# Splitting every fourth half unit of streamed weights with two GpSimd DMAs in a two-block transformer kernel

## Chip, cores and metric

The kernel runs on one core of one Trainium2 chip. The metric is the device time of that core in microseconds, as the median over runs of the same program. All inputs lie in the chip's memory before the program starts, and the output is written back there.

## What is computed

The reference applies two transformer blocks to 256 tokens of width 2048, in float32. Block 1 has differential attention and retention side by side, then cross attention to 256 memory tokens, then a gated feed-forward. Block 2 has spatial gating and a gated linear recurrence side by side, then a feed-forward with a short convolution. All the large work is the matrix products with the weights:

```python
def first_block(x, mem, ...):
    h = rmsnorm(x, norm_mix_g[l]);  proj = h @ w_in[l]
    ...                                   # differential attention, retention -> mixed
    x = x + mixed @ w_o[l]
    hx = rmsnorm(x, norm_x_g[l]);  hm = rmsnorm(mem, norm_mem_g[l])
    xq, xk, xv = hx @ w_xq[l], hm @ w_xk[l], hm @ w_xv[l]
    ...                                   # softmax attention -> xo
    x = x + xo @ w_xo[l]
    hf = rmsnorm(x, norm_ffn_g[l])
    x = x + (silu(hf @ w_gate[l]) * (hf @ w_up[l])) @ w_down[l]
    return rmsnorm(x, norm_f_g)

def second_block(x, ...):
    p = rmsnorm(x, norm1_g[l]) @ w_in[l]
    ...                                   # spatial gating, recurrence -> y
    x = x + y @ w_out[l]
    up = causal_dwconv(rmsnorm(x, norm2_g[l]) @ ffn_w_up[l])
    gate, val = split(up)
    x = x + (gelu(gate) * val) @ ffn_w_down[l]
    return rmsnorm(x, final_g)
```

## The kernel before

Every product is computed with split operands: a float32 value is written as hi + lo, both of type float32r, where hi is the value cast to float32r and lo is what the cast left over. A product then is hi·hi + hi·lo + lo·hi, three matmuls in place of one, added up in PSUM.

The weights are a stream. They lie in memory as 452 units of 1 MB, each 128 partitions by 2048 floats, in the order `seq` in which the GEMMs use them. `fetch` (lines 218 to 226) loads one unit on the SP queue into a tile `w` of the pool `wraw` (3 buffers). `push` (line 228) takes a half unit, 128 by 1024, from it and calls `split` (line 127). There ACT casts it into a tile `wh` of the pool `whi` (line 129), and DVE subtracts `wh` from the raw weights into a tile `wl` of the pool `wlo` (line 130). Each of these two pools has 5 buffers. So half unit n takes the buffers that half unit n−5 had, and can start only when PE has done the last matmul with that one. There are 904 half units; the last 5 are kept in other tiles for a second pass, so 899 go through `wh` and `wl`.

`half` (line 249) is called by the GEMMs for the next half unit and keeps `LOOKAHEAD` = 4 further ones pushed. `gemm_tm` (line 312) has the activations as stationary operand and moves 512 weight columns: for one half unit 4 groups of the three matmuls of `mm3`, lines 145 (hi weights), 146 (lo weights) and 147 (hi weights). `gemm_fm` (line 282) has the weights as stationary operand: 8 matmuls with hi weights against 512 columns (line 297) and 8 with lo weights against 256 (line 301) for one half unit. PSUM holds two groups at a time (`pg`).

Work beside the GEMMs (attention heads, norms, the recurrence) is written as generators, one stage per half unit (`tick`, line 262). A scheduler then sets the order of the instructions on each engine from estimated durations; each engine takes its list strictly in that order and waits where an operand or a buffer is not ready. POOL, the engine of GpSimd, has little to do: inverse square roots by power (line 151), some additions of squares (line 413) and two selections (line 828).

Of the kernel before, what the change touches and what calls it, by code (L numbers as in the profile page):

```python
# [8 lines left out]
F32 = mybir.dt.float32  # L9
F32R = mybir.dt.float32r  # L10
# [12 lines left out]
LOOKAHEAD = 4  # L23
TAIL = 5  # half units at the end whose operands stay for a second pass

# columns of the packed per-feature vectors
_COLS = [
# [17 lines left out]
def tile_kernel(ctx, tc, x, xT, mem, memT, par, alibi, rdecay, ident_d, bc_rows, gm_wsT,  # L45
# [29 lines left out]
    class Pair:  # L75
        """two k-tiles of a split operand: tiles of (hi | lo), or a tile of hi and one of lo"""

# [13 lines left out]
        def fill(self, src, gcols=None):  # L91
            """hi + lo == src * gain; src [P, 2, S] or two of [P, S]"""
            if gcols is None and not self.joined:
                split(self.t[0], self.t[1], src)
            else:
                for k in range(2):
                    split(self.hi(k), self.lo(k), src[:, k, :], None if gcols is None else gcols[k])
            return self
# [6 lines left out]

# [1 line left out]
    pr = cpool.tile([P, NPAR], F32, name="pr")  # L107
# [6 lines left out]
    V.memset(mhalf, -0.5)  # L114
    # the first activation table loads while the first data comes
    A.activation(st(1), mhalf[:, 0:1], AF.Square)
# [8 lines left out]

# [1 line left out]
    def split(hi, lo, src, gcol=None):  # L127
# [7 lines left out]
    def xpose_split(src, c, gcols=None, joined=False):  # L135
        """token-major src[t][:, c:c+256] -> split feature-major pair"""
        pt = sps().rearrange("p (k s) -> p k s", k=2)
        for k in range(2):
            for t in range(2):
                T.transpose(pt[:, k, t * P:(t + 1) * P], src[t][:, c + k * P:c + (k + 1) * P], ident)  # L140
        return Pair(joined).fill(pt, gcols)

    def mm3(out, lh, rh, start, stop):
        """both operands as (hi, lo)"""
        T.matmul(out, lhsT=lh[0], rhs=rh[0], start=start, stop=False)  # L145
        T.matmul(out, lhsT=lh[0], rhs=rh[1], start=False, stop=False)  # L146
        T.matmul(out, lhsT=lh[1], rhs=rh[0], start=False, stop=stop)  # L147
# [6 lines left out]
    class Sq:  # L154
        """sums of squares of token-major rows, piece by piece"""

# [18 lines left out]
    def rows(c):  # L175
        """[P tokens, 2] columns -> [P, 256], the same row in every partition"""
        d = flat(ft())[:, 0:S]
        for t in range(2):
            V.tensor_scalar(d[:, t * P:(t + 1) * P], ident, c[:, t:t + 1], None, ALU.mult)
        ps = sps()  # L180
        T.matmul(ps[:, 0:S], lhsT=ones, rhs=d, start=True, stop=True)
        r = spool.tile([P, S], F32, tag="rows", name=nm("rows"), bufs=3)
        A.copy(r, ps[:, 0:S])
        return r
# [3 lines left out]

# [1 line left out]
    seq = [(w_in_f, 0, u) for u in range(2)]  # L190
# [37 lines left out]
    def push():  # L228
        """one more half unit on its way"""
        w, g, u = seq[pos[1] // 2]  # L230
        h = pos[1] % 2
        if not raws:
            fetch()
        r = raws[0][:, 1024 * h:1024 * h + 1024]
        if h == 1:
            raws.pop(0)
        pos[1] += 1
        if pos[1] > 2 * len(seq) - TAIL:
            # kept until both halves of the tokens have used them
            hi, lo = [flat(rt()) for _ in range(2)], [flat(rt()) for _ in range(2)]  # L240
            for k in range(2):
                split(hi[k], lo[k], r[:, 512 * k:512 * k + 512])
        else:
            hi = whi.tile([P, 1024], F32R, tag="h", name=nm("wh"))
            lo = wlo.tile([P, 1024], F32R, tag="l", name=nm("wl"))
            split(hi, lo, r)
        feed.append((w, g, u, h, hi, lo))
# [10 lines left out]

# [1 line left out]
    bg = []  # L260
# [21 lines left out]
    def gemm_fm(wap, g, acts):  # L282
        """256 output features x 256 tokens: [P, m, (hi parts | lo parts)]"""
        ps = psg.tile([P, 2, 512], F32, tag="g", name=nm("pg"))
# [27 lines left out]
    def gemm_tm(wap, g, acts, k0=0, ps=None, tail=0):  # L312
        """256 tokens (2 banks) x 512 output features; in the last `tail` half units the second
        half of the tokens waits for the function that is returned"""
        if ps is None:
# [39 lines left out]
    def evac_split(ps, c):  # L355
        """token-major, as (hi, lo) for each half of the tokens"""
        res = []
        for t in range(2):
            hi, lo = flat(rt()), flat(rt())
            split(hi, lo, ps[t], need(c, 0)[:, t:t + 1])  # L360
            res.append((hi, lo))
        return res
# [10 lines left out]
    def operands(g, acts, gcols):  # L373
        """columns 512 g of the residual as operands of a GEMM"""
        for p in range(2):
# [4 lines left out]
    def next_in(g, acts, sq, gcols, after=None):  # L380
        """behind a residual update of columns 512 g"""
        if acts is not None:
# [8 lines left out]
    def stats(sq, rc, rr=None):  # L391
        """rstd of the rows as columns, and as a row in every partition"""
        rc[0] = sq.rstd(D)
# [4 lines left out]

    # =================================================================
    # block 1: projections, differential attention, retention  # L400
    # =================================================================
    def load(src, p):
# [4 lines left out]
    def load_split(f, gname, p, sq):  # L407
        a = Pair(True).fill(f, [col(gname, 2 * p + j) for j in range(2)])
        # sum of squares, feature-major
        s = ft()  # L410
# [7 lines left out]
    def col_stats(sq, n):  # L418
        """feature-major squares -> rstd as columns"""
        tot = sps()  # L420
# [10 lines left out]
    def x_gen():  # L431
        # loads (L), weight units (W) and splits (S) in the order in which they start
        n = 0
# [26 lines left out]

    # lambda = exp(q1.k1) - exp(q2.k2) + lam_init
    lam_init = 0.8 - 0.6 * math.exp(-0.3 * 0)
# [17 lines left out]
    def av_stage(pT, v, off):  # L480
        """[q, 256] = P^T.T @ v, causal in blocks of 128, and its sums of squares"""
        po = sps().rearrange("p (t e) -> p t e", t=2)
# [123 lines left out]

    # memory
    hm_a, sqm = [None] * 8, []
# [29 lines left out]

    # =================================================================
    # cross attention  # L640
    # =================================================================
    xk = []
# [6 lines left out]
    for g in range(4):  # L649
        if g == 3:  # L650
            # takes the space of the memory's operands, pair by pair
            spawn(chain([operands(i, hx_a, cols("norm_x_g", 0, 16)) for i in range(4)]))
# [50 lines left out]

    # =================================================================
    # feed-forward 1
    # =================================================================
    gg = cpool.tile([P, 16], F32, name="gg")
# [9 lines left out]
    def second_norm(g):  # L717
        # block 2 takes rmsnorm(x) * norm_f_g and normalises it again
        gf = flat(ft())
# [20 lines left out]

    # =================================================================
    # block 2: spatial gating and recurrent branch
    # =================================================================
    def tok(ins):
        # one order for the functions that share no activation table
        tc.stamp_issue_order_token(ins.ins, "tables")
        return ins
# [18 lines left out]

    # softplus(-lam) = max(-lam, 0) + log1p(exp(-|lam|))
    c8 = cpool.tile([P, 2, 8], F32, name="c8")
# [26 lines left out]
    def v_norm(t):  # L795
# [13 lines left out]
        for g in range(2):  # L809
            V.scalar_tensor_tensor(vg[t][g], vg[t][g], rr, gvg[g], ALU.mult, ALU.mult)  # L810
            V.tensor_tensor(vg[t][g], vg[t][g], gvb[g], ALU.add)
            yield
        # mixing over tokens, token-major
        for g in range(2):
# [10 lines left out]
    for f in ws:  # L825
        # keep s <= t
        f3 = f.rearrange("p (h t) -> p h t", t=P)
# [20 lines left out]

# [1 line left out]
    wa, wx = big(lru_wa), big(lru_wx)  # L850
# [29 lines left out]
    def lru_scan():  # L880
        for p in range(4):
# [5 lines left out]
            yield  # L887
            # 1 - exp(-2z) = tanh(z) * (1 + exp(-z)^2)
            d_ = ft()
# [84 lines left out]

    # =================================================================
    # feed-forward 2
    # =================================================================
    def conv3(z, c0):
# [36 lines left out]

    # last columns: the first half of the tokens leaves while the second is computed
    ps = [sps(), sps()]
# [98 lines left out]
```

## Time and profile before

| what | value |
|---|---|
| median of 2 runs | 2611.34 us (2611.17 to 2611.5) |
| span of the profiled execution | 2611.1 us |
| DVE busy on line 130, 899 subtractions | 1101.4 us |
| ACT busy on line 129, 899 casts | 944.1 us |
| memory read in the span | 486.39 MB, 187 GB/s |
| mean granted clock of TensorE | 0.999 |

The profile is of one execution. PE is the matmul engine, PEld its load of the stationary operand, DVE the vector engine, ACT the scalar engine, POOL GpSimd, SP the engine that issues the loads. A row of a group gives the line of the kernel, the engine, the operation with output and inputs, the count, then busy time and mean duration in nanoseconds of one, then the idle time of the engine ahead of these instructions and what ended most of it. A row of issues gives the engine whose queue it is, the count, the size of one and the median time from issue to landing. A row of a timeline gives start and duration in microseconds, and in brackets the idle time ahead of it and what ended it. Matmuls overlap in the pipeline, so the distance between two starts, not the duration, is what one costs. The rows themselves stand in the prediction, where they are used.

### The profile page before, as it was taken

To read this page: it belongs to the slowest core of one execution; us is meant where nothing else is said; L and a number is where in the kernel's file an instruction comes from. 1 tells how busy PE (TensorE), PEld (TensorE's weight loads), DVE (VectorE), ACT (ScalarE), POOL (GpSimd) and SP (SyncE) were. 2 spreads that over 40 slices of the span, in tenths; PEclk is the share of its full clock that TensorE was granted. 3 is DMA by queue.
4 is the path that set the end of the run, shared out by engine and by line. 5 is a ranking of instruction groups with operands and counts; after the bars stand their busy time and mean duration, and the time that the engine had idled before them with its cause. 6 is when DMAs were issued, how large, how long until landed. Compare 5 with 4: busy or idle time off the path is not lost.

```text
span 2611.1 us, 32123 instructions
## 1 busy us (share of the span) xinstructions
PE 2590.6 (99%) x12922; PEld 2192.4 (84%) x12922; DVE 1575.4 (60%) x1889; ACT 1292.5 (50%) x1683; POOL 38.1 (1%) x41
## 2 busy tenths in 40 slices
PE   8999999999999999999999999999999999999998
PEld 7888888888888888888888888888888888888887
DVE  6665565556555454545454557866777745777754
ACT  5555554454454444334444555755555534555543
POOL 1000010000000000000000000000000000000000
PEclk9999999999999999999999999999999999999999
DMA  6455555554455555555555555554555555555563
GB/s 245 172 177 202 200 203 185 187 184 157 158 177 186 188 191 193 191 193 187 188 192 193 199 200 190 178 193 177 192 181 188 185 193 190 194 182 189 180 215 137
DMA packets 72726, 490.57 MB, mean 188 GB/s; under 512 B 8193, under 2 KB 8321, under 8 KB 14593
## 3 DMA queue, kind: packets, MB, share of 16 engines
q1 hardware_dynamic: 72576, 488.52, 53.2%
q8 instruction: 101, 1.65, 0.2%
q14 instruction: 49, 0.39, 0.0%
HBM read 486.39 MB, written 2.10 MB: 187 GB/s over the span
## 4 chain that ended last, share of the span: by engine, by line
PE 98%; issue 0%; DVE 0%; ACT 0%; DMA 0%; POOL 0%; SPq 0%; ACTq 0%; POOLq 0%; DVEq 0%
PE pg L297 24%; PE pg L145 19%; PE pg L146 19%; PE pg L147 19%; PE pg L301 12%; PE pp L140 1%; PE pp L147 1%; PE pp L146 1%; PE pp L145 1%; DMA w<-in_w_in_f_dram 0%; DVE r L133 0%; PE pp L818 0%; PE pp L871 0%; PE pp L870 0%; ACT junk L163 0%
## 5 line engine op out<-in xcount | busy, mean ns | idle before, releaser
L130 DVE TENSOR_TENSOR wl<-w,wh 128x1024 fp32r<-128x1024 f32 x899 | 1101.4, 1226 | 840.9 <-ACT wh L129 836.1
L129 ACT CAST wh<-w 128x1024 fp32r<-128x1024 f32 x899 | 944.1, 1051 | 983.2 <-PE pg L147 737.6
L297 PE MATMUL pg<-r,wh 128*128 128x512 f32 x2688 | 945.8, 401 | 12.0 <-ACT wh L129 7.3
L145 PE MATMUL pg<-wh,r 128*128 128x512 f32 x2224 | 870.2, 391 | 0.0
L147 PE MATMUL pg<-wh,r 128*128 128x512 f32 x2224 | 867.9, 390 | 0.0
L146 PE MATMUL pg<-wl,r 128*128 128x512 f32 x2224 | 867.5, 390 | 0.0
L301 PE MATMUL pg<-r,wl 128*128 128x256 f32 x2688 | 731.3, 283 | 0.5 <-DVE wl L130 0.5
L297 PEld LDWEIGHTS pg<-r,wh 128*128 128x128 f32 x2688 | 497.1, 189 | 120.0 <-ACT wh L129 7.3
L301 PEld LDWEIGHTS pg<-r,wl 128*128 128x128 f32 x2688 | 510.6, 190 | 17.6 <-DVE wl L130 1.0
L147 PEld LDWEIGHTS pg<-wh,r 128*128 128x128 f32 x2224 | 417.8, 188 | 86.4
L146 PEld LDWEIGHTS pg<-wl,r 128*128 128x128 f32 x2224 | 418.0, 188 | 85.6 <-DVE wl L130 0.4
L145 PEld LDWEIGHTS pg<-wh,r 128*128 128x128 f32 x2224 | 417.8, 188 | 84.4
L343 DVE TENSOR_TENSOR f<-pg,f 128x512 f32<-128x512 f32 x84 | 58.0, 691 | 90.2 <-ACT f L342 90.2
L342 ACT COPY f<-pg 128x512 f32<-128x512 f32 x84 | 49.2, 586 | 125.4 <-PE pg L297 125.4
L985 DVE SCALAR_TENSOR_TENSOR f<-f,pr,f 128x255 f32<-128x255 f32 x192 | 79.9, 478 | 0.7 <-ACT f L982 0.7
L982 ACT ACTIVATE f<-f,pr 128x256 f32<-128x256 f32 x96 | 52.6, 595 | 26.2 <-DVE f L344 26.1
L344 DVE TENSOR_TENSOR f<-f,rows 128x512 f32<-128x512 f32 x84 | 58.1, 691 | 2.6
L129 ACT CAST r<-f 128x512 fp32r<-128x512 f32 (+1 forms) x56 | 34.1, 610 | 16.3 <-DVE f L344 12.5
L371 DVE TENSOR_TENSOR xt<-xt,pg 128x512 f32<-128x512 f32 x54 | 34.7, 684 | 10.5 <-PE pg L147 10.5
L151 POOL TENSOR_TENSOR s<-s,mhalf 128x2 f32<-128x2 f32 (+1 forms) x21 | 14.3, 680 | 1783.0 <-DVE s L1026 802.7
L163 ACT ACTIVATE junk<-xt 128x512 f32<-128x512 f32 x48 | 30.2, 628 | 18.2 <-DVE xt L1022 17.2
L146 PE MATMUL pp<-r,r 128*128 128x256 f32 (+2 forms) x132 | 39.1, 299 | 0.0
(163 smaller groups left out, 860.8 us busy)
## 6 DMA issues: line engine op xcount, KB each, us to landing
w<-in_w_up_dram SPq DMA_DIRECT2D x140, 1024.0 KB, 4.8
w<-in_w_down_dram SPq DMA_DIRECT2D x92, 1024.0 KB, 4.8
w<-in_w_gate_dram SPq DMA_DIRECT2D x44, 1024.0 KB, 4.8
w<-in_w_in_t_dram SPq DMA_DIRECT2D x40, 1024.0 KB, 4.8
w<-in_w_in_f_dram SPq DMA_DIRECT2D x39, 1024.0 KB, 4.8
w<-in_w_o_dram SPq DMA_DIRECT2D x16, 1024.0 KB, 4.8
w<-in_w_xk_dram SPq DMA_DIRECT2D x16, 1024.0 KB, 4.8
w<-in_w_xv_dram SPq DMA_DIRECT2D x16, 1024.0 KB, 4.8
```

The lines of the kernel that those rows point to most:

```text
L129: A.copy(hi, src)
L130: V.tensor_tensor(lo, src, hi.bitcast(F32), ALU.subtract)
L145: T.matmul(out, lhsT=lh[0], rhs=rh[0], start=start, stop=False)
L146: T.matmul(out, lhsT=lh[0], rhs=rh[1], start=False, stop=False)
L147: T.matmul(out, lhsT=lh[1], rhs=rh[0], start=False, stop=stop)
L297: T.matmul(ps[:, m, :], lhsT=hi[k][:, ms], rhs=a.both(k % 2), start=first, stop=last, skip_group_check=True)
L301: T.matmul(ps[:, m, S:], lhsT=lo[k][:, ms], rhs=a.hi(k % 2), start=False, stop=False, skip_group_check=True)
L342: A.copy(f, ps[:, :, S:])
L343: V.tensor_tensor(f, ps[:, :, 0:S], f, ALU.add)
L344: V.tensor_tensor(f, f, bc2(need(r, 0)), ALU.mult)
L982: A.activation(y[:, j, :], z[:, j, :], AF.Identity, scale=col("ffn_conv_w_2", 192 + c), bias=col("ffn_conv_b_2", c))
L985: V.scalar_tensor_tensor(y[:, j, d:], z[:, j, :S - d], col("ffn_conv_w_2", 96 * (2 - d) + c), y[:, j, d:], ALU.mult, ALU.add)
```

## The change

In `push`, every fourth half unit (the second half of every other unit, 224 in all) no longer calls `split`. Its hi is written by a DMA on the GpSimd queue straight from memory, from float32 into the float32r tile `wh`. ACT then writes −hi into the tile `wl`. A second DMA on the GpSimd queue reads the same weights from memory again and adds them onto `wl`, which leaves w − hi. The load of the whole raw unit on SP remains; of the changed half of it nothing is read. The other three of four half units are made as before. The remaining lines of the diff remove comments and docstrings, which shifts line numbers by up to 8: line 413 becomes 421, line 351 becomes 359; the new ones are 248 (hi), 249 (negation) and 250 (lo).

```diff
         else:
             hi = whi.tile([P, 1024], F32R, tag="h", name=nm("wh"))
-            lo = wlo.tile([P, 1024], F32R, tag="l", name=nm("wl"))
-            split(hi, lo, r)
+            if pos[1] % 4 == 0:
+
+                lo_ = wlo.tile([P, 1024], F32R, tag="l", name=nm("wl"))
+                G.dma_start(out=hi, in_=w[g, u][:, 1024 * h:1024 * h + 1024])
+                A.activation(lo_, hi.bitcast(F32), AF.Identity, scale=-1.0)
+                G.dma_start(out=lo_, in_=w[g, u][:, 1024 * h:1024 * h + 1024], accum_op=ALU.add)
+                lo = lo_
+            else:
+                lo = wlo.tile([P, 1024], F32R, tag="l", name=nm("wl"))
+                split(hi, lo, r)
         feed.append((w, g, u, h, hi, lo))
```

The new instructions also change the order that the scheduler finds. Three places show how. All are in the first part of feed-forward 1, around half units 311 to 319 of the stream. The numbers in tile names are running numbers of the tiles, and they differ between the two kernels; half units 311 to 319 have the tiles wh_7495, 7513, 7529, 7547, 7563, 7586, 7602, 7620 and 7636 before, and wh_7572, 7591, 7607, 7625, 7641, 7665, 7681, 7699 and 7715 in the changed kernel. In both, the number of a `wl` is that of its `wh` plus one. Changed are 311, 315 and 319.

The list of POOL before, from the last additions for the memory's norm to the selections in block 2; feed-forward 1 lies between the last two kinds:

```order
L413 TENSOR_TENSOR f_2816<-f_2816,f_3015 128x512
L151 TENSOR_TENSOR s_3077<-s_3075,mhalf 128x2
L151 TENSOR_TENSOR s_3606<-s_3603,mhalf 128x2
L151 TENSOR_TENSOR s_6683<-s_6680,mhalf 128x2
L828 AFFINE_SELECT f_11451<-f_11451 128x512
```

The list of POOL in the changed kernel, half units 311, 315, 319, 323 and 327 (only the hi of the last):

```order
L248 DMA wh_7572<-in_w_gate_dram 128x1024
L250 DMA wl_7573<-in_w_gate_dram 128x1024
L248 DMA wh_7641<-in_w_up_dram 128x1024
L248 DMA wh_7715<-in_w_up_dram 128x1024
L250 DMA wl_7642<-in_w_up_dram 128x1024
L250 DMA wl_7716<-in_w_up_dram 128x1024
L248 DMA wh_7784<-in_w_gate_dram 128x1024
L250 DMA wl_7785<-in_w_gate_dram 128x1024
L248 DMA wh_7874<-in_w_gate_dram 128x1024
```

Where POOL had nothing, it now has two transfers for every fourth half unit. Mostly hi and lo of one follow each other; for half unit 315 the lo stands behind the hi of 319. That is so for 16 of the 224.

The list of ACT before, half units 312 to 320, with the evacuation of a gate product between them:

```order
L129 CAST wh_7513<-w_7511 128x1024
L129 CAST wh_7529<-w_7511 128x1024
L129 CAST wh_7547<-w_7545 128x1024
L129 CAST wh_7563<-w_7545 128x1024
L351 ACTIVATE f_7579<-pg_7424,s_6683 128x512
L351 ACTIVATE f_7581<-pg_7424,s_6683 128x512
L129 CAST wh_7586<-w_7584 128x1024
L129 CAST wh_7602<-w_7584 128x1024
L129 CAST wh_7620<-w_7618 128x1024
L129 CAST wh_7636<-w_7618 128x1024
```

The same stretch of ACT in the changed kernel:

```order
L129 CAST wh_7591<-w_7589 128x1024
L129 CAST wh_7607<-w_7589 128x1024
L249 ACTIVATE wl_7573<-wh_7572 128x1024
L129 CAST wh_7625<-w_7623 128x1024
L129 CAST wh_7665<-w_7663 128x1024
L359 ACTIVATE f_7658<-pg_7501,s_6750 128x512
L359 ACTIVATE f_7660<-pg_7501,s_6750 128x512
L129 CAST wh_7681<-w_7663 128x1024
L129 CAST wh_7699<-w_7697 128x1024
L249 ACTIVATE wl_7642<-wh_7641 128x1024
L249 ACTIVATE wl_7716<-wh_7715 128x1024
```

The casts stand in the order of the half units. The negation of 311 stands behind the casts of 312 and 313, that of 315 behind those of 316, 317 and 318. Over the whole program 116 negations stand behind two later casts, 65 behind one, 21 behind three, and 22 behind none.

The list of PE before, from the end of half unit 311 into 312:

```order
L145 MATMUL pg_7424<-wh_7495,r_6569 128x512
L146 MATMUL pg_7424<-wl_7496,r_6569 128x512
L147 MATMUL pg_7424<-wh_7495,r_6569 128x512
L145 MATMUL pg_7583<-wh_7513,r_6058 128x512
L146 MATMUL pg_7583<-wl_7514,r_6058 128x512
L147 MATMUL pg_7583<-wh_7513,r_6058 128x512
```

The same place in the changed kernel, from the end of 310 into 311 and 312:

```order
L145 MATMUL pg_7501<-wh_7556,r_6623 128x512
L146 MATMUL pg_7501<-wl_7557,r_6623 128x512
L147 MATMUL pg_7501<-wh_7556,r_6623 128x512
L145 MATMUL pg_7662<-wh_7591,r_6117 128x512
L145 MATMUL pg_7501<-wh_7572,r_6633 128x512
L146 MATMUL pg_7662<-wl_7592,r_6117 128x512
L147 MATMUL pg_7662<-wh_7591,r_6117 128x512
L145 MATMUL pg_7662<-wh_7591,r_6118 128x512
```

Before, PE takes one half unit after the other. Now it does one matmul of 311, then all of 312 and nine of the twelve of 313, which belong to the next PSUM group, and only then the first that reads wl_7573 and the rest of 311. Such exchanges stand at many, not all, of the changed half units; 315 is taken in its place.

## The prediction

> **What bounds the kernel now.** I read the page first: busy times, then the chain that ended last, then the costliest groups.
>
> ```profile
> span 2611.1 us, 32123 instructions
> PE 2590.6 (99%) x12922; PEld 2192.4 (84%) x12922; DVE 1575.4 (60%) x1889; ACT 1292.5 (50%) x1683; POOL 38.1 (1%) x41
> ...
> q1 hardware_dynamic: 72576, 488.52, 53.2%
> ...
> PE 98%; issue 0%; DVE 0%; ACT 0%; DMA 0%; POOL 0%; SPq 0%; ACTq 0%; POOLq 0%; DVEq 0%
> ...
> L130 DVE TENSOR_TENSOR wl<-w,wh 128x1024 fp32r<-128x1024 f32 x899 | 1101.4, 1226 | 840.9 <-ACT wh L129 836.1
> L129 ACT CAST wh<-w 128x1024 fp32r<-128x1024 f32 x899 | 944.1, 1051 | 983.2 <-PE pg L147 737.6
> ...
> L151 POOL TENSOR_TENSOR s<-s,mhalf 128x2 f32<-128x2 f32 (+1 forms) x21 | 14.3, 680 | 1783.0 <-DVE s L1026 802.7
> ```
>
> PE is busy 2590.6 of 2611.1 us and carries 98% of the chain. The two splitting engines idle: ACT spends 983 us ahead of its casts, mostly because PE has not yet freed a buffer. So no work taken from DVE or ACT can gain more than 2611.1 − 2590.6 = 20.5 us, 0.8%. What can change the time is a PE wait that is not there today.
>
> The timeline of feed-forward 1 shows the rhythm against which every new latency is to be held.
>
> ```profile
> 1300.95 0.39 PE L147 MATMUL pg<-wh,r 128*128 128x512 f32 x1
> ...
> 1301.18 0.39 PE L145 MATMUL pg<-wh,r 128*128 128x512 f32 x1
> ...
> 1301.38 1.05 ACT L129 CAST wh<-w 128x1024 fp32r<-128x1024 f32 x1 [1.66 <-PE pg L147]
> ...
> 1302.46 1.22 DVE L130 TENSOR_TENSOR wl<-w,wh 128x1024 fp32r<-128x1024 f32 x1 [1.49 <-ACT wh L129]
> ...
> 1304.10 1.05 ACT L129 CAST wh<-w 128x1024 fp32r<-128x1024 f32 x1 [1.67 <-PE pg L147]
> ```
>
> A half unit takes 1304.10 − 1301.38 = 2.72 us, 12 matmuls of 0.227 us. The cast starts 0.04 us behind the end of the old half unit's last matmul (1300.95 + 0.39), thus 0.20 us into the next one, and hi and lo are ready 2.3 us later. With five buffers they are needed only four half units, 10.9 us, after the release, so some 8.5 us are spare. In the other kind of GEMM (256 features by 256 tokens) a 512-column row is followed 0.23 us later by a 256-column row, and that one 0.12 us later by the next, which makes 2.8 us a half unit:
>
> ```profile
> 2008.31 0.40 PE L297 MATMUL pg<-r,wh 128*128 128x512 f32 x1
> ...
> 2008.54 0.28 PE L301 MATMUL pg<-r,wl 128*128 128x256 f32 x1
> ...
> 2008.66 0.40 PE L297 MATMUL pg<-r,wh 128*128 128x512 f32 x1
> ```
>
> **The change, step by step.** *Removed:* 224 of 899 casts and 224 subtractions. DVE loses 224 × 1.226 = 275 us; ACT's 224 casts become 224 negations of the same shape, at 1.05 us each, so ACT is even. Both are off the path: 0 us.
>
> *Kept:* every 1 MB load on SP. *Added:* 448 transfers of 0.52 MB on POOL's queue, 235 MB. At today's 53.2% for 488.5 MB that is +25.6%, to 79% of the rings; if the adding one also moves its destination, +12.8% more, 92%. Full, but below the bound.
>
> *The new chain* for a changed half unit n is: buffer n−5 released, hi lands (H), negation 1.05 us, lo lands (L), first matmul that reads wl. No POOL transfer stands in this trace, so H and L are bounded by the nearest issues:
>
> ```profile
> w<-in_w_up_dram SPq DMA_DIRECT2D x140, 1024.0 KB, 4.8
> ...
> f<-in_xT_dram SPq DMA_DIRECT2D x8, 256.0 KB, 7.8
> ...
> out_dram<-xt SPq DMA_DIRECT2D x8, 256.0 KB, 2.4
> w<-in_w_in_f_dram SPq DMA_DIRECT2D x2, 512.0 KB, 5.1
> ...
> pr<-in_par_dram SPq DMA_DIRECT2D x1, 8.0 KB, 1.7
> ```
>
> How fast full rings move data, and what a waiting PE does to its clock (used below), stands in the windows of the first microseconds (columns: length; PE, PEld, DVE, ACT, POOL busy; granted clock, DMA share, GB/s):
>
> ```profile
> 17.00:19.00 2.00, 0.61 (x2) 0.30 (x2) 2.00 (x4) 2.00 (x3) 1.56 (x2) 1.00 1.02 425
> 19.00:21.00 2.00, 1.80 (x7) 1.57 (x8) 2.00 (x5) 2.00 (x6) 0.74 (x1) 0.66 1.04 415
> 21.00:23.00 2.00, 2.00 (x8) 1.71 (x8) 2.00 (x3) 1.20 (x2) 2.00 (x1) 0.50 0.71 295
> 23.00:25.00 2.00, 2.00 (x13) 1.75 (x12) 2.00 (x2) 0.29 (x1) 1.72 (x2) 0.99 0.89 246
> ```
>
> Low end: 1 MB lands in 4.8 us; its data at 425 GB/s needs 2.5 of these, so half of it would land in 3.6 us on free rings. High end: 7.8 us, the row of loads that met full rings at the start (share 1.02). I take H = 5.1, the one row of this very size, which also shared its rings; and L = 6.3, as the add must fetch its destination too (0.52 MB at 425 GB/s, 1.2 us, an estimate).
>
> *Where the wait falls* is decided by the lists. ACT takes the negation behind casts of later half units (in the excerpt of ACT: wl_7573 behind those of n+1 and n+2, the commonest case), and the cast of n+2 waits for the release of n−3. From that release it is 0.20 + 1.05 (cast) + 1.05 (negation) + 0.05 = 2.35 us until lo can be issued, then L. Against it stands the lead: the PE work listed between that release and the first row that reads wl, at 0.227 us per 512-column row and 0.118 per 256-column row. Stall = 2.35 + L − lead, with L = 6.3 the threshold is 8.65 us. The scheduler lengthens many leads itself, as the PE excerpt shows: one row of n, then n+1, then the rest. Counted over all 224:
>
> - 13 units whose lo stands on POOL behind the hi transfer of n+4, which waits for the release of n−1: lo is issued as n begins. Stall 6.4 each: 83 us.
> - 6 with leads of 0.3 us on average: 8.3 each, 50 us. 6 of 2.6: 6.0 each, 36 us.
> - 8 of 4.3: 35 us. 23 of 5.8: 66 us. 49 of 6.75: 93 us.
> - 19 around 8.55: about 0.3 each, 5 us. 100 of over 9: nothing from this.
>
> That is 368 us. The same chain from hi: 0.2 + H + 1.05 + 0.15 + L = 12.8 us against the lead from release of n−5, which is 11.1 us for 65 units; where the wait above was not already that long it adds 1.7 us, in sum 45 us. Together 413 us.
>
> *Two edits priced at nothing:* the square roots on POOL (21, 14.3 us) now stand behind transfers that wait up to one half unit; the background heads they belong to have a half unit or more between stages, and without that cover it would be 21 × 2.72 = 57 us. The evacuations on ACT behind a negation that waits for hi: hi lands 5.3 us after its release, ahead of the n+2 cast (6.7), so nothing queues; beyond H = 6.5 every excess lengthens the classes above.
>
> *What is late next* is the clock. In the windows above PE idles 1.4 of 2 us, then runs at half clock for about 3.3 us, which loses 1.6 us. I charge that to the 33 stalls above 3.4 us: 53 us. The low bound is 0; the high one, all 117 stalls, 187 us.
>
> Sum: 2611.1 (span) + 413 + 53 = 3077; since a stalled PE also thins out the traffic, a little less, 3060 us. The span stands 0.2 us below the median of 2611.34.
>
> The Trainium skill, "DMA: Bandwidth & Descriptors", section "Anatomy of one DMA — SWDGE (gpsimd) path", gives 2.0 us plus bytes over 436 GB/s for a transfer of this kind, 3.2 us for 0.52 MB, without cast or add; by it the sum would be some 105 us, an estimate, and the time 2715. The 1 MB row agrees roughly (4.4 by the rule, 4.8 measured); no run here shows the rule for a cast or an add.
>
> **Rivals.**
>
> *Short landings.* H and L of 3.6 to 4.8: the same classes give 119 to 226 us, 2730 to 2840. For it speaks that rings are busy only half the time; against it the 5.1 and 7.8 us of smaller loads.
>
> *The rings fill.* If cast and add cost twice a plain byte, the added 25.6% become 51.2%, together 104% of the old span: H = 6.3 to 7.8 and L near 9. Then the classes up to 11 us stall too: 867 to 1106 us, with the clock 3480 to 3750. For it: 79% without any such penalty; against it: a stalled PE also spaces out the loads.
>
> *The clock drops after every stall.* 117 × 1.6 = 187 in place of 53: 3200. For it: 1.4 us of idling sufficed at 17 us; against it: stalls of 2 us in 11 leave PE busy 80%. The Trainium skill, "TensorE: Matmul & The Clock Gate", Part 1, says the clock halves after an idle window of about 3.4 us and returns after a busy one as long; by that rule only long stalls count, and the trace's 3.3 us of recovery agree.
>
> *Not slower.* The lo transfer lands so early that only the 25 shortest leads see it. With L = 1.7 us, the 8 KB row, these cost 13 × 1.8 + 6 × 3.7 + 6 × 1.4 = 54 us, 2665; from there down it is no measurable change. A 64 times larger transfer in that time is hardly to be had, and faster than 2560 is shut out by PE's own 2590.6.
>
> **How the numbers follow.** My forecast (2840 to 3300) 0.52; short landings 0.17; rings full 0.20; clock after every stall 0.06; not slower 0.05. The range leaves out "not slower" and the upper half of the full rings: 2740 to 3550. A measurement of this kernel can tell about 2% from no change: slower by over 2% 0.95, within 0.04, faster 0.01.
>
> **What would show it.** Right: PE busy falls well below 90%, PE waits named after the DMA of wl at the matmuls of L146 and L301, about 115 waits with a long group near 6 us; POOL issues landing near 5 and 6 us; granted clock below 1 after long waits. Wrong: landings under 4 us, or a queue share near 100% with waits on hi, or waits of PE on DVE's wl instead, which would mean that blocked casts, not lo, are late.

## The result and the profile after

The changed kernel takes 3395.27 us (median of 2 runs, 3390.65 to 3399.88) where the kernel before takes 2611.34: a ratio of 1.2996, 95% interval 1.2975 to 1.3018. That is 784 us slower; the forecast was 449 us slower.

The page of the changed kernel, the lines that answer to those quoted in the prediction:

```profile
span 3398.2 us, 32708 instructions
PE 2804.9 (83%) x12922; PEld 2310.2 (68%) x12922; DVE 1309.6 (39%) x1665; ACT 1266.8 (37%) x1683; POOL 364.9 (11%) x489
...
q1 hardware_dynamic: 72576, 488.52, 39.2%
q0 software_dynamic: 64512, 234.91, 29.5%
...
L130 DVE TENSOR_TENSOR wl<-w,wh 128x1024 fp32r<-128x1024 f32 x675 | 819.2, 1225 | 1333.9 <-ACT wh L129 1329.7
L146 PE MATMUL pg<-wl,r 128*128 128x512 f32 x2224 | 939.5, 423 | 460.1 <-DMA wl<-in_w_up_dram 130.5
...
w<-in_w_up_dram SPq DMA_DIRECT2D x140, 1024.0 KB, 7.2
...
wh<-in_w_up_dram POOLq DMA_DIRECT2D x70, 512.0 KB, 8.9
wl<-in_w_up_dram POOLq DMA_DIRECT2D x70, 512.0 KB, 5.7
```

PE does the same 12922 matmuls, but its share falls from 99% to 83%. DVE's 224 subtractions are gone (1101.4 to 819.2 us on line 130) and bought nothing. The idle time of L146, the matmul that reads wl, is 460.1 us, and it ends mostly with the adding DMA. The raw loads, untouched by the change, land in 7.2 us in place of 4.8. ("Rings" here are the 16 DMA engines that move all transfers; their share is the last figure of a queue's row.)

The span grew by 3398.2 − 2611.1 = 787 us. PE was busy 2804.9 − 2590.6 = 214 us longer, so it was idle 573 us longer. What it waited for (engine, tile and line of the waiter; releaser; sum, times, longest, in us):

```profile
PE pg L146 <- DMA wl<-in_w_up_dram: 130.5, 11, 12.6
PE pg L146 <- DMA wl<-in_w_down_dram: 117.1, 33, 12.1
PE pg L146 <- DMA wl<-in_w_gate_dram: 71.0, 20, 9.3
PE pg L146 <- DMA wl<-in_w_in_t_dram: 55.3, 11, 11.6
PE pg L309 <- DMA wl<-in_w_up_dram: 32.9, 26, 4.0
```

In the whole list the adding DMA ends 533 us of PE's waits. Only 3 us end with the casting DMA of wh. Of the 11 waits in `in_w_up` at L146, 130.5 us in sum and most of the longest, nine are of half units whose lo stands on POOL behind the next hi. One of these nine, first POOL, then ACT and SP (start, duration, idle ahead and its end):

```profile
1106.06 0.55 POOL L248 DMA_DIRECT2D wh<-in_w_up_dram  x1 [12.89 <-PE pg L147]
1106.80 0.89 POOL L250 DMA_DIRECT2D wl<-in_w_up_dram  x1 [0.18 <-issue]
1116.31 0.88 POOL L250 DMA_DIRECT2D wl<-in_w_up_dram  x1 [8.63 <-ACT wl L249]
...
1105.44 1.06 ACT L249 ACTIVATE wl<-wh 128x1024 fp32r<-128x1024 f32 x1
...
1105.88 1.46 SPq L224 DMA_DIRECT2D w<-in_w_gate_dram  x2
```

PE at the same place:

```profile
1105.59 0.39 PE L145 MATMUL pg<-wh,r 128*128 128x512 f32 x1
1118.47 0.80 PE L146 MATMUL pg<-wl,r 128*128 128x512 f32 x1 [12.49 <-DMA wl<-in_w_up_dram]
```

And the windows (length; PE, PEld, DVE, ACT, POOL busy; granted clock, DMA share, GB/s):

```profile
1106.00:1108.00 2.00, 0.00 (x0) 0.00 (x0) 0.99 (x1) 0.50 (x1) 1.44 (x2) 1.00 0.53 123
1108.00:1110.00 2.00, 0.00 (x0) 0.00 (x0) 0.00 (x0) 0.00 (x0) 0.00 (x0) 0.56 1.00 410
1110.00:1112.00 2.00, 0.00 (x0) 0.00 (x0) 0.00 (x0) 0.00 (x0) 0.00 (x0) 0.50 1.01 240
...
1118.00:1120.00 2.00, 1.53 (x4) 1.25 (x5) 0.00 (x0) 0.00 (x0) 0.00 (x0) 0.50 0.87 137
1120.00:1122.00 2.00, 2.00 (x7) 1.59 (x6) 0.00 (x0) 0.00 (x0) 0.00 (x0) 0.53 0.58 113
```

PE starts the half unit at 1105.59 and wants its lo one row later. The lo is issued only at 1106.80, behind a hi that waited for the buffer PE had just released, and together with two raw loads. POOL's order is not what made it late: its negation, behind two casts on ACT, ended at 1106.50, and a lo goes out 0.3 us after its negation elsewhere too (median 0.29 us). In all 16 half units with this exchange lo was issued 0.3 to 0.9 us after its negation. The rings are full for 10 us, the lo lands 11.6 us after its issue, PE waits 12.49 us, and its clock is at half from 1108 to beyond 1120: the first matmul afterwards takes 0.80 us in place of 0.39. Over the rest of the program this repeats in smaller sizes.

### The profile page after: what moved, and what is told of

Same layout as the page of the kernel before. It is cut to its first block, busy times and chain, and to the rows that moved or that the text cites. A ratio compares the mean times of both kernels' runs of the same rounds, so it can differ in the third digit from the quotient of the medians.

```text
span 3398.2 us, 32708 instructions
## 1 busy us (share of the span) xinstructions
PE 2804.9 (83%) x12922; PEld 2310.2 (68%) x12922; DVE 1309.6 (39%) x1665; ACT 1266.8 (37%) x1683; POOL 364.9 (11%) x489
## 3 DMA queue, kind: packets, MB, share of 16 engines
q1 hardware_dynamic: 72576, 488.52, 39.2%
## 4 chain that ended last, share of the span: by engine, by line
issue 48%; PE 24%; DMA 18%; POOL 5%; DVE 2%; ACT 2%; POOLq 0%; SPq 0%; ACTq 0%; DVEq 0%
PE pg L146 7%; PE pg L147 6%; PE pg L145 6%; DMA wl<-in_w_up_dram 4%; PE pg L305 3%; DMA wl<-in_w_down_dram 3%; POOL wl L250 2%; DMA wl<-in_w_gate_dram 2%; POOL wh L248 2%; DVE wl L130 2%; PE pg L309 2%; DMA wl<-in_w_in_t_dram 2%; ACT wh L129 2%; DMA wl<-in_w_xo_dram 1%; DMA wl<-in_w_o_dram 1%
## 5 line engine op out<-in xcount | busy, mean ns | idle before, releaser
L130 DVE TENSOR_TENSOR wl<-w,wh 128x1024 fp32r<-128x1024 f32 x675 | 819.2, 1225 | 1333.9 <-ACT wh L129 1329.7
L146 PE MATMUL pg<-wl,r 128*128 128x512 f32 x2224 | 939.5, 423 | 460.1 <-DMA wl<-in_w_up_dram 130.5
L129 ACT CAST wh<-w 128x1024 fp32r<-128x1024 f32 x675 | 702.9, 1050 | 1276.4 <-PE pg L147 864.4
L147 PE MATMUL pg<-wh,r 128*128 128x512 f32 x2224 | 921.2, 415 | 0.0
L145 PE MATMUL pg<-wh,r 128*128 128x512 f32 x2224 | 911.7, 413 | 3.2 <-DMA wh<-in_w_in_t_dram 2.6
L146 PEld LDWEIGHTS pg<-wl,r 128*128 128x128 f32 x2224 | 453.4, 204 | 592.9 <-DMA wl<-in_w_up_dram 135.1
L145 PEld LDWEIGHTS pg<-wh,r 128*128 128x128 f32 x2224 | 450.4, 203 | 105.0 <-DMA wh<-in_w_in_t_dram 3.0
L147 PEld LDWEIGHTS pg<-wh,r 128*128 128x128 f32 x2224 | 453.9, 204 | 95.2
L249 ACT ACTIVATE wl<-wh 128x1024 fp32r<-128x1024 f32 x224 | 237.0, 1058 | 360.4 <-DMA wh<-in_w_up_dram 212.4
L250 POOL DMA_DIRECT2D wl<-in_w_up_dram x70 | 60.5, 865 | 606.1 <-ACT wl L249 480.2
L250 POOL DMA_DIRECT2D wl<-in_w_down_dram x44 | 37.8, 860 | 443.0 <-ACT wl L249 257.3
L248 POOL DMA_DIRECT2D wh<-in_w_up_dram x70 | 42.3, 604 | 199.6 <-PE pg L147 150.4
```

Of the source, the lines that this page charges most:

```text
L129: A.copy(hi, src)
L130: V.tensor_tensor(lo, src, hi.bitcast(F32), ALU.subtract)
L248: G.dma_start(out=hi, in_=w[g, u][:, 1024 * h:1024 * h + 1024])
L249: A.activation(lo_, hi.bitcast(F32), AF.Identity, scale=-1.0)
L250: G.dma_start(out=lo_, in_=w[g, u][:, 1024 * h:1024 * h + 1024], accum_op=ALU.add)
```

## The experiments

**Theory A, latency against lead:** hi and lo land one after the other inside a lead of about four half units (10.9 us), and what the landings exceed it by, PE waits. **Theory B, the rings:** 235 MB more are more than they carry at this pace. **Theory C, the lists:** the place of the negation on ACT and of lo on POOL alone makes the waits. Diffs are against the changed kernel. Landing times in the text, where no row shows them, are means over a kernel's own issues in its trace; "PE idle" is the idle time ahead of PE's instructions, "half clock" the time at a granted clock of 0.5, both of the profiled execution.

### Each part alone

Hi by DMA, lo by DVE as before:

```diff
-                A.activation(lo_, hi.bitcast(F32), AF.Identity, scale=-1.0)
-                G.dma_start(out=lo_, in_=w[g, u][:, 1024 * h:1024 * h + 1024], accum_op=ALU.add)
+                V.tensor_tensor(lo, r, hi.bitcast(F32), ALU.subtract)
```

> Only the casting transfer stays: hi by GpSimd DMA, lo by DVE from the raw weights as before the change. Latency against lead (theory A: a transfer lands about 8 us after its issue because the raw loads share its rings, and PE waits when that exceeds the lead its place in the lists gives it): 0.2 us to the issue, 8 us to land, 1.2 us on DVE, 9.4 of 10.9 us, so few waits: 2611 to 2700 us. Ring throughput (theory B: the added bytes fill the rings): 117 of the 235 MB and the cheap part, some 0.3 of the added 784 us: 2850. Order alone (theory C: negation and lo stand too late on ACT and POOL, the landings matter little): 2611 to 2650, not told apart from A here.

Measured: 2620.81 us, ratio 1.0031 (1.0020 to 1.0042). From its page, the shares of the two queues (loads of SP are q1, GpSimd's q0) and the landing of hi (last column):

```profile
q1 hardware_dynamic: 72576, 488.52, 50.6%
q0 software_dynamic: 32256, 117.45, 13.9%
...
wh<-in_w_up_dram POOLq DMA_DIRECT2D x70, 512.0 KB, 5.0
```

Lo by the adding DMA, hi cast by ACT as before:

```diff
-                G.dma_start(out=hi, in_=w[g, u][:, 1024 * h:1024 * h + 1024])
+                A.copy(hi, r)
```

> Only the adding transfer stays: hi by ACT from the raw weights, then the negation on ACT, then the adding DMA. From the release 0.2 + 1.05 + 1.05 + 0.05 = 2.35 us to the issue, 5.4 us to land when alone and up to 8 beside raw loads: 7.8 to 10.4 of 10.9 us. Theory A: 2611 to 2750. Theory B: the add has 0.7 of the added ring time (387 against 174 ns a packet): 3000 to 3150. Theory C: every negation stands right behind its own cast, so 2611 to 2650.

Measured: 2625.05 us, ratio 1.0050 (1.0031 to 1.0070). The same lines of its page:

```profile
q1 hardware_dynamic: 72576, 488.52, 53.9%
q0 software_dynamic: 32256, 117.45, 24.1%
...
wl<-in_w_up_dram POOLq DMA_DIRECT2D x70, 512.0 KB, 6.6
```

Either transfer alone costs 0.3 to 0.5%; together they cost 30%. So neither transfer makes the loss by itself, and B's 2850 and 3000 fail; A and C both allow these times. The queue shares also price a byte: raw 53.2% × 2611.1 / 488.52 = 2.84 us of ring time per MB before, the cast 13.9% × 2616.3 / 117.45 = 3.10, the add 24.1% × 2624.5 / 117.45 = 5.39. The add costs nearly two plain transfers, as if it moved its destination too.

### The add made a plain write

```diff
-                G.dma_start(out=lo_, in_=w[g, u][:, 1024 * h:1024 * h + 1024], accum_op=ALU.add)
+                G.dma_start(out=lo, in_=w[g, u][:, 1024 * h:1024 * h + 1024])
```

> The changed kernel with the second DMA overwriting wl in place of adding onto it, so lo holds w and the output is not the reference's; the lists of all engines stay as they are. Theory A: landing of lo falls by about 1.6 us alone (128 packets of 4 KB at 174 in place of 387 ns on 16 engines), on 132 waits 210 us, with the slow clock behind them some 300: 3050 to 3150. Theory B: ring time of the POOL queue falls by a third, 350 us: 3050, not told apart from A here. Theory C: the lists are the same, so over 3300.

Measured: 3102.0 us, ratio 1.1876 (1.1820 to 1.1931). Lo lands in 5.6 us in place of 7.6, hi in 7.2 in place of 8.1. So the adding itself carries 293 of the 784 us; 491 us remain with two landings in series and no add. The time is inside A's range and close to B's 3050; C's "over 3300" fails.

### The lists

Hi held behind the lo before it on POOL, so that no lo stands behind a later hi:

```diff
+                if order[0] is None:
+                    G.dma_start(out=hi, ...)
+                else:
+                    with tc.issue_after(order[0].ins):
+                        G.dma_start(out=hi, ...)
...
+                order[0] = G.dma_start(out=lo, ..., accum_op=ALU.add)
```

> The changed kernel with each hi transfer held behind the lo transfer before it on POOL, so that none of the 16 exchanges is left; the place of the negations on ACT stays nearly the same. Theories A and C: the 13 waits of 12.4 us become waits of about 5, 13 x 7.4 = 96 us, and about 40 us less at half clock: 3220 to 3290. Theory B: the bytes are the same, within 40 us of 3395.

Measured: 3351.98 us, ratio 1.2833 (1.2796 to 1.2870): a gain of 43 us, less than half of the low end expected. Nine waits of 10.6 to 11.8 us remain, all in `in_w_up`. There lo is issued 4.5 to 4.8 us after its hi has landed, as POOL waits for the negation, and lands 9.7 to 11.0 us later. So POOL's order is not the main thing; in these units ACT's list sets when lo goes out.

The same, and each cast on ACT held behind the negation before it, so that no negation stands behind a later cast:

```diff
+                order[1] = A.activation(lo, hi.bitcast(F32), AF.Identity, scale=-1.0)
...
-                split(hi, lo, r)
+                if order[1] is None:
+                    split(hi, lo, r)
+                else:
+                    with tc.issue_after(order[1].ins):
+                        split(hi, lo, r)
```

> The changed kernel with every later cast held behind the negation on ACT, and every hi behind the lo before it on POOL. The chain then runs from the release of the buffer alone: 0.2 + hi 5 to 8 + 1.2 + lo 5.4 to 7 = 11.8 to 16.4 us against 10.9 us, which the order on PE stretches by up to 5 in places. Theory A: waits of 1 to 4 us in about half of the 224 units, with the clock 2750 to 2950. Theory C (place of the negation alone): 2611 to 2680. If neither the lists nor the series matter, near 3395.

Measured: 2977.77 us, ratio 1.1401 (1.1368 to 1.1434), 28 us above the range expected. The lists carry more than half of the loss (418 of 784 us), so C is a large part and not the whole. From its page, PE's share and the wait at L146:

```profile
PE 2707.7 (91%) x12922; PEld 2243.5 (75%) x12922; DVE 1292.4 (43%) x1665; ACT 1246.0 (42%) x1683; POOL 354.7 (12%) x489
...
L146 PE MATMUL pg<-wl,r 128*128 128x512 f32 x2224 | 904.7, 407 | 183.1 <-DMA wl<-in_w_down_dram 56.1
```

With these lists a lo goes out 1.5 us (median) after its hi has landed. The chain left is, with mean landings, 0.2 + 7.2 (hi) + 1.5 + 5.8 (lo) = 14.7 us against 10.9. It is over 10.9 us in all 224 units, and yet only 108 make PE wait, 226 us in sum: the others must have a longer lead, as PE's list can give it. So the chain against 10.9 us gives the direction of a change, not its size.

### Bytes against the chain

The same 235 MB, but cast and add on different half units, so that no half unit has both landings:

```diff
+                V.tensor_tensor(lo, r, hi.bitcast(F32), ALU.subtract)
+            elif pos[1] % 4 == 2:
+                lo = wlo.tile([P, 1024], F32R, tag="l", name=nm("wl"))
+                A.copy(hi, r)
+                A.activation(lo, hi.bitcast(F32), AF.Identity, scale=-1.0)
+                G.dma_start(out=lo, ..., accum_op=ALU.add)
```

> The same 235 MB by as many casting and as many adding transfers, but on different half units: of four, one gets hi by a casting DMA (lo by DVE), another lo by an adding DMA (hi and the negation by ACT). No half unit has the two in series. Theory A (a chain of two landings against a lead of 10.9 us): each chain stays under 10.9 us as it did alone, so the two costs of about 9 and 13 us plus some for fuller rings: 2630 to 2720. Theory B (ring throughput): the bytes and packets of the changed kernel, so near 3395, at the least over 3200.

Measured: 3042.53 us, ratio 1.1649 (1.1595 to 1.1703). Both theories missed. From its page, busy times, queues and landings:

```profile
PE 2724.9 (90%) x12922; PEld 2259.5 (74%) x12922; DVE 1300.7 (43%) x1664; ACT 1279.8 (42%) x1684; POOL 357.5 (12%) x490
...
q1 hardware_dynamic: 72576, 488.52, 44.5%
q0 software_dynamic: 64656, 235.43, 32.5%
...
wl<-in_w_up_dram POOLq DMA_DIRECT2D x70, 512.0 KB, 8.7
wh<-in_w_up_dram POOLq DMA_DIRECT2D x70, 512.0 KB, 8.2
```

A had taken the landings from the two runs with one kind of transfer (4.8 and 7.0 us on average). With both kinds in the program they became 8.0 and 7.8. Against the lead: where the negation stands behind its own cast, lo has landed 0.20 + 1.05 + 1.05 + 0.30 + L after the buffer's release. In the run with lo alone, that is the place of 223 of 224 negations, and nine in ten L are under 8.2 us: 10.8 us, just inside 10.9. Here the median L is 8.4 and one in ten is over 10.2, and 65 of 225 negations stand a half unit later. So the chain in series is not needed for a loss; the transfers lengthen each other.

All half units split by ACT and DVE, and the same 448 transfers into a spare tile that no matmul reads:

```diff
+                if spare[0] is not None:
+                    V.tensor_copy(spare[1], spare[0][:, 0:1].bitcast(F32))
+                x_ = wsp.tile([P, 1024], F32R, tag="x", name=nm("wx"))
+                G.dma_start(out=x_, in_=w[g, u][:, 1024 * h:1024 * h + 1024])
+                G.dma_start(out=x_, in_=w[g, u][:, 1024 * h:1024 * h + 1024], accum_op=ALU.add)
+                spare[0], spare[1] = x_, st(1)
```

> Every half unit is split on ACT and DVE as before the change; the same 448 transfers (224 casting, 224 adding, 235 MB) go into a spare tile that no matmul reads, with a one-column copy on DVE that frees it. Theory A (two landings in series against the lead of a few half units): nothing waits for these transfers, the raw loads land in some 7 us but have three buffers, so 2611 to 2680 us. Theory B (the rings carry no more): the time stays near that of the changed kernel, above 3200 us.

Measured: 2864.42 us, ratio 1.0973 (1.0951 to 1.0995). A and B both missed again. From its page, busy times, queues, the matmul that reads wl (here L148) and the copy that frees the spare tile (L252):

```profile
PE 2666.1 (93%) x12922; PEld 2219.5 (77%) x12922; DVE 1569.5 (55%) x2112; ACT 1276.9 (45%) x1685; POOL 358.1 (13%) x489
...
q1 hardware_dynamic: 72576, 488.52, 46.6%
q0 software_dynamic: 64512, 234.91, 35.4%
...
L148 PE MATMUL pg<-wl,r 128*128 128x512 f32 x2224 | 882.3, 397 | 69.6 <-DVE wl L132 69.0
...
L252 DVE COPY s<-wx 128x1 f32<-128x1 f32 x223 | 32.8, 152 | 779.6 <-DMA wx<-in_w_up_dram 279.2
```

The run has a flaw of its own: the copy that frees the spare tile made DVE wait 779.6 us for landings, with the subtractions queued behind it. Of PE's 188 us of waits over 0.3 us, 169 had DVE held at that copy within the 9 us before; such stretches cover some 55% of the span, so this is a hint and not a proof. If the held copy only adds time, 253 us is an upper bound for what the traffic alone costs. That suffices against B: the rings carried all the bytes at a share of 46.6 + 35.4 = 82% in 2864 us, and were 69% busy in the changed kernel's 3398. Their time is the same in both (82.0% × 2864.4 = 2349, 68.7% × 3398.2 = 2335 us): the changed kernel leaves them idle while it waits.

### Dose, lead and bytes

Every eighth half unit (112):

```diff
-            if pos[1] % 4 == 0:
+            if pos[1] % 8 == 0:
```

> Every eighth half unit (112) is made by the two transfers. Theory A: half as many chains, landings shorter than at every fourth (hi near 6, lo near 6.5 us), so under half of the loss of 784 us: 2800 to 3000 us. Theory B (rings): with half of the added bytes the rings are far from full, so nearly nothing is lost: under 2700 us.

Measured: 2847.9 us, ratio 1.0902 (1.0885 to 1.0918). Half the dose leaves 236 of 784 us, inside A's range, and B's "under 2700" fails at a ring share of 65%. The transfers of different changed half units no longer overlap here, and yet hi lands in 6.9 us: 83 of 112 hi start with two raw loads in flight.

Six buffers and five half units pushed ahead:

```diff
-LOOKAHEAD = 4
+LOOKAHEAD = 5
...
-    whi = ctx.enter_context(tc.tile_pool(name="whi", bufs=5))
-    wlo = ctx.enter_context(tc.tile_pool(name="wlo", bufs=5))
+    whi = ctx.enter_context(tc.tile_pool(name="whi", bufs=6))
+    wlo = ctx.enter_context(tc.tile_pool(name="wlo", bufs=6))
```

> The changed kernel with six buffers in place of five for wh and for wl and five half units pushed ahead (four buffers of the other pool given up for the room). Every lead grows by one half unit, 2.7 us; the lists hold 20 exchanges on POOL and 35 negations behind three casts. Theory A: 132 waits get up to 2.7 us shorter, about 250 us of waits and 80 at half clock less: 3000 to 3150. Theory B: same bytes, within 60 us of 3395. Theory C: the lists are no better, so the same or slower than 3395.

Measured: 3218.2 us, ratio 1.2321 (1.2254 to 1.2389), 68 us above the range. The scheduler spends part of the added lead: 35 negations now stand behind three later casts where 21 did, and 20 lo behind a later hi where 16 did; hi lands in 8.5 us.

The unused half of each raw unit not loaded:

```diff
+            if pos[0] % 2 == 1 and 2 * pos[0] + 2 <= 2 * len(seq) - TAIL:
+                c = slice(0, 1024)
```

> The changed kernel without the half of every other raw unit that nothing reads: 117 MB less on SP's queue, the result unchanged. Theory A with raw loads as what delays the landings: hi lands 1 to 2 us earlier and the lists come out with 2 exchanges in place of 16, so 3000 to 3200. Theory B: 117 of 726 MB less ring time, 16% of it: 2850 to 2950. If raw loads do not delay the landings and the lists are what matters: 3250 to 3350 from the exchanges alone, since removing these gave 43 us.

Measured: 3204.12 us, ratio 1.2268 (1.2229 to 1.2306). 117 MB less gain 191 us, 4 us short of A's range; lo lands in 6.6 us in place of 7.6. The lists changed with it (2 exchanges on POOL for 16, 2 negations behind three casts for 21), so not all of the gain need be the traffic.

### The best version of the change

Ordered lists and half loads together:

> The negation ahead of the later casts, the hi transfer behind the lo before it, and the unused half of a raw unit not loaded. Theory A (chain against lead, landings lengthened by the traffic beside them): the 2978 us of the ordered lists fall by about the share that leaving out the half load gave on the lists of the changed kernel (191 of 784), to 2820 to 2920 us. A rival, that only the raw load issued in the same burst as the hi transfer delays it: under 2750 us.

Measured: 2947.67 us, ratio 1.1295 (1.1260 to 1.1331): 30 us less than with the ordered lists alone, where A expected 60 to 160. On these lists lo lands in 5.6 us, and what is left is hi (6.8 us) in series with it.

The same with six buffers:

> As the kernel with ordered lists and half loads, but with six buffers for wh and wl in place of five and five half units pushed ahead. Theory A: the lead grows by a half unit, 2.72 us, in all chains, so most waits vanish: 2650 to 2800 us; the 2590.6 us that PE was busy before the change is the floor, so it does not beat the kernel before. If instead the landings grow with the depth, as in the run with six buffers alone: 2800 us or more.

Measured: 2741.61 us, ratio 1.0485 (1.0458 to 1.0512). From its page, busy times and landings:

```profile
PE 2637.8 (96%) x12922; PEld 2200.2 (80%) x12922; DVE 1282.8 (47%) x1665; ACT 1236.7 (45%) x1683; POOL 357.5 (13%) x489
...
w<-in_w_up_dram SPq DMA_DIRECT2D x70, 1024.0 KB, 7.6
w<-in_w_up_dram SPq DMA_DIRECT2D x70, 512.0 KB, 5.0
wh<-in_w_up_dram POOLq DMA_DIRECT2D x70, 512.0 KB, 6.6
wl<-in_w_up_dram POOLq DMA_DIRECT2D x70, 512.0 KB, 5.5
```

The landings are those of the run with five buffers (hi 6.9, lo 5.7 on average), and the lead grew by a half unit, 2.72 us: the chain is 0.2 + 6.9 + 1.5 + 5.7 = 14.3 us against 13.6, where it was 14.1 against 10.9. Only 67 units make PE wait, where 115 did, and 206 us are gone: the clearest sign of latency against lead. It still does not beat the kernel before.

| kernel | us | hi, lo landing | PE idle | half clock |
|---|---|---|---|---|
| changed | 3395.27 | 8.1, 7.6 | 585 | 609 |
| hi alone | 2620.81 | 4.8, – | 18 | 7 |
| lo alone | 2625.05 | –, 7.0 | 21 | 17 |
| apart | 3042.53 | 8.0, 7.8 | 302 | 266 |
| ordered lists | 2977.77 | 7.2, 5.8 | 261 | 197 |
| ordered, half loads | 2947.67 | 6.8, 5.6 | 247 | 202 |
| ordered, half loads, six buffers | 2741.61 | 6.9, 5.7 | 109 | 57 |

The account that the runs leave is A with an amendment: what PE waits is the chain (landings, negation, place in the lists) less the lead, and the landings are not constants but grow with what is in flight when they are issued. How long the lead of each half unit is, the runs do not give, so the size of the loss is not worked out from it. The gains of the parts do not add: the plain write 293, the ordered lists 418, the half loads 191 on the lists of the changed kernel and 30 on ordered ones, because each shortens the same waits, and a wait that is gone cannot be shortened again. What the traffic alone costs without any chain stays open, likely below the 253 us of the flawed run.

## Why the prediction was right, and what it mis-sized

**Bound and removed work: right.** DVE's 282 us on line 130 were worth nothing, and every microsecond of change is PE's: 573 idle, 214 of slower matmuls.

**The mechanism: right.** PE waits at the matmuls that read wl, for the adding DMA, and hardly for hi; PE is at 83% (forecast: well below 90); the clock falls after long waits. There are 120 waits of over 1 us, 110 of them for lo, where about 115 were named; but the long group is near 12 us, not near 6.

**Ring load: right.** The rings work 2335 us, 89% of the old span; the two bounds were 79%, and 92% if the add moves its destination.

**H = 5.1 and L = 6.3: too small.** On average hi took 8.1 us and lo 7.6. On idle rings the casting transfer lands in 3.9 us and the adding one in 5.4, and alone in the program they took 4.8 and 7.0, so the rows chosen were fair for one transfer. The failed step is that they were taken from a program without the other transfers. In the changed kernel a hi that had another GpSimd transfer in flight 0.5 us after its issue took 8.8 us (151 of them), without one 6.5 (73); a lo with no raw load in flight then (each counted from the end of its own issue) took 6.2 (92), with one 8.3 (114), with two 9.9 (18). A smaller error of the same kind: lo goes out 0.3 us after its negation, where 0.05 was put. The rule of the Trainium skill, "DMA: Bandwidth & Descriptors", section "Anatomy of one DMA — SWDGE (gpsimd) path", gave 3.2 us; the measured 3.9 and 5.4 on idle rings are both above it, as is a plain write on GpSimd's queue (3.9 us, 11 on idle rings in the run without the add), and the time it led to, 2715, was far off. The 1 MB row that the prediction held against the rule is of a load on SP's queue, not of this path.

**The exchanged half units, 13 × 6.4 = 83 us: half the size.** The kernel has 16 such half units; 12 of them wait 11.6 to 12.6 us each, 148 us, the other four 6 us together. The class was found, but its lo was given the L of a lone transfer: it leaves together with a hi and raw loads and lands 11.4 to 12.1 us after its issue. That the place on POOL sets the issue was wrong, too: the negation held it as long, to within 0.7 us, and with POOL's order put right the time fell by 43 us only.

**The other waits, 330 us: nearly right in sum.** The remaining waits on lo are 533 − 155 = 378 us. With landings 1 to 3 us longer than assumed, the classes should have given more; that a wait also gives time to the half units in flight behind it would explain it, but no run isolates this. The hi chain, 45 us in the sum, was not isolated either; with ordered lists it is the only chain left, and PE is idle 261 us.

**The clock, 53 us: a quarter of the size.** PE was busy 214 us longer. The trace has 86 stretches at half clock, 609 us. Of the waits of 0.7 to 1 us none of 14 is followed by one, of 1 to 2 us 3 of 28, of 2 to 3 us 12 of 20, of 3 to 4 us 9 of 9, of longer ones 62 of 63. The limit of 3.4 us was too high, and each stretch lost 214/86 = 2.5 us in place of 1.6. The rival "after every stall" (187 us) came nearer in size, though short waits do not do it. The Trainium skill, "TensorE: Matmul & The Clock Gate", Part 1, has the clock fall after an idle window of about 3.4 us; the trace agrees on the length of the stretches (85 of 86 are multiples of 3.41 us), but waits of 2 to 3 us were already enough in 12 of 20 cases. The 1.4 us of idling that the prediction read at 17 us in the kernel before are parts of two waits, 0.92 and 1.02 us, with work between them; so idle time may add up over a few us, which no run isolates.

**The edits priced at nothing: nearly so.** PE's waits for anything but these transfers rose from 13 us to about 49; the square roots behind transfers had a bound of 57.

**The rivals.** Short landings fell with H and L; from the class averages their upper end is 206 us, not 226. The 867 to 1106 us of the full rings cannot be worked out again from the classes listed, and their 3480 has nothing for the clock in it. "The rings fill" had the landings nearly right (6.3 to 7.8, near 9) and its range began at 3480, but its reason is only half true: the rings are full within a burst, as in the window above, and 69% busy over the span. The error of the sum, 3060 against 3395, is about 160 us of waits and 160 us of clock.

## What to carry to other kernels

Where a stream is split just in time, the price of a DMA in place of an engine's instruction is its landing against the lead, not the engine time it saves; its bytes count through the landings that they lengthen. Two landings in series need a lead of both. A deeper lookahead took 177 us off the changed kernel and 206 us off the one with ordered lists and half loads, but only the latter came within 5% of the kernel before. Take the landing from a run in which all the new transfers are in flight, since one kind at a time (0.3 and 0.5% here) tells nothing of both (30%). And work taken from an engine with slack, before a bound engine at 99%, has nothing to give.

## What the hardware showed unexpectedly

An adding GpSimd transfer from memory into float32r keeps the rings busy some 1.7 times as long as a plain or casting one: on quiet rings its 4 KB packets took 377 ns (mean of seven transfers of the changed kernel), those of a casting one 215 (five, hi alone) and those of a plain write 216 (11, without the add). It also holds POOL longer at issue, 0.86 against 0.56 us.

A transfer issued in a burst with raw loads starts late: the first packet of a hi came 1.25 us after its issue on quiet rings, but 3.5 us in the median with every eighth half unit changed, where mostly two raw loads were in flight. In the run with hi alone it came after 1.3 us with one raw load in flight (148 transfers) and after 3.0 us with two (69). The Trainium skill, "DMA: Bandwidth & Descriptors", section "Issuing engines are not separate DMA queues", says that transfers of all issuing engines run on the same 16 engines and interleave; this delay of the first packet shows that here a later transfer still waited for much of what was issued before it; where on its way it waits, the trace does not tell.
